# A fourth raw tile, later weight stores, and a tile for the second token tile beside the output weights

## The chip, the cores and the metric

The kernel runs on one core of a Trainium2 chip. The core has five engines that run at the same time, each with its own stream of instructions: TensorE (PE in the profile) multiplies matrices, VectorE (DVE) and GpSimd (POOL) do elementwise work, ScalarE (ACT) evaluates functions and copies, SyncE (SP) issues most transfers. The transfers themselves are done by 16 DMA engines. The metric is the device time of one execution in microseconds, the median of several runs; less is better.

## The reference

One layer of a hybrid backbone on 2048 latent tokens of width 1024, with a context of 256 tokens in front. Everything is in 32-bit floating point. Cut to what matters here:

```python
ada = jnp.einsum('bd,lde->lbe', jax.nn.silu(c), w_ada) + b_ada[:, None, :]
sh1, sc1, g1, sh2, sc2, g2 = (m[:, None, :] for m in jnp.split(ada[l], 6, axis=-1))
...
hc = modulate(rmsnorm(xc, norm_mix[l]), csh1, csc1)
logf_f, k_f, logf_b, k_b, vc = hgrn2_gates(hc @ w_in[l][:, :3 * w], lb_f, lb_b, first)
hf_c = advance_state(h0, k_f, vc, jnp.cumsum(logf_f, axis=2))
hb_c = advance_state(h0, flip_t(k_b), flip_t(vc), jnp.cumsum(flip_t(logf_b), axis=2))

h = modulate(rmsnorm(x, norm_mix[l]), sh1, sc1)
o, _, _ = token_mixers(h @ w_in[l], lb_f, lb_b, first, hf_c, hb_c, *mix_args)
x = x + g1 * (o @ w_out[l])
h2 = modulate(rmsnorm(x, norm_ffn[l]), sh2, sc2)
x = x + g2 * conv_ffn(h2, w_up[l], conv_w[l], conv_b[l], w_down[l], rows)
return rmsnorm(x, norm_final)
```

`token_mixers` has two groups of four heads. One is a gated linear recurrence that runs over the tokens forward and backward, each direction starting from the state that the context leaves. The other is a gate unit: `gelu(u) * (W_s LN(gelu(v)) + b)` over chunks of 128 positions. Their outputs are joined and go through `w_out`.

## The kernel before

Products that need accuracy are made of three multiplications: each operand is split into a high part in the rounded format float32r and the rest (`split`, L131: a cast on ACT, a subtraction on DVE or POOL), and `mm3` (L136) multiplies high by high, high by low and low by high.

The kernel has three phases.

Phase one (L192 to L1162) makes the input projection, the recurrences and the gate unit. It takes the tokens in two halves of 1024 (`hh` 0 and 1). `run_banks` (L525) goes through a list of column tiles of `w_in`; each is a product of 128 columns by up to 512 tokens in one PSUM bank. The 512 KB of weights of a column tile are loaded into a *raw tile* (`raw_tile`, L214: 4 KB in each partition, three of them) by `load_raw` (L219), and split into `whi` and `wlo` by `split_w` (L224), for which there are two pairs. Between the multiplications of a bank, `slot` (L185) lets two queues of background tasks go on. A task is a generator; what it yields is the number of microseconds of PE time, by the planner's own estimate in `Tensor` (L54), after which it goes on. The queue `hg_q` holds the recurrences of the heads. The queue `bg_q` holds, one after the other: the normalising of x, `ada_block` for the rest of the modulation (L951), `w_out_ops` (L982), `conv_taps`, `w_down_ops` (L998), and at the end `load` in `open_wo` (L1136).

`w_out_ops` has 16 steps. Each takes a raw tile, loads half a row block of `w_out` (L991), yields 8.0, multiplies by the gate `g1` on DVE (L993), splits, stores the result in DRAM (L995), and yields 1.5. `w_down_ops` has 22 steps: load (L1006), yield 8.0, multiply (L1008), store (L1009), yield 2.0. Both share the raw tiles with the projection weights. Nearly all transfers of the kernel are issued by SP, in program order: where SP waits for the data of a store, or for a tile to come free, all later transfers wait behind it.

The last projection banks of phase one belong to the gate unit. Its last step, `both` (L682), multiplies on POOL (L685) and stores to `oT_d` in DRAM (L686). Before the last four banks, `open_wo` (L1127) empties the queues, closes the pool `ph` of the recurrence, and opens `pw` in its place. Its `load` fetches the joined outputs of token tile 0 (L1138) and the prepared output weights, half by half (L1144), and splits token tile 0 some 17 us of PE time later (L1147).

Phase two (L1273 to L1374) is the output projection over 16 token tiles of 128 tokens, with the residual and the second norm. Tile `t` needs its joined outputs fetched (`fetch_o`, L1313) and split (`split_o`, L1319), 48 multiplications into a pair of PSUM banks (`dbank`, L1192), and its rows of x (`fetch_x`, L1324). Before the loop, tile 1 is fetched (L1329) and then the first rows of x (L1330).

After it come the up-projection with the convolution, and the down-projection with the final norm. The last is the only place of `root` (L1719) with a column as its second operand (L1749): the rows' mean square and a constant are added on POOL, and the power -0.5 is taken. PSUM has eight banks; each phase lays its own pool over them, in the order in which tags are first asked for.

Of the kernel before, what the change touches and what calls it, by code (L numbers as in the profile page):

```python
# [18 lines left out]
P = 128  # L19
D = 1024  # L20
# [63 lines left out]
def tile_trunk(ctx, tc, x, c, cx, c_ctx, w_ada, b_ada, norm_mix, norm_ffn, w_in, hg_norm, sgu_g, sgu_b,  # L84
# [15 lines left out]
    ones = cst.tile([P, P], F32, name="ones")  # L100
    G.memset(ones, 1.0)
    ones_r = cst.tile([P, P], F32R, name="ones_r")
    nc.gpsimd.tensor_copy(ones_r, ones)
# [87 lines left out]
    with es1:  # L191
# [5 lines left out]
        wa = [p1.tile([P, NK, TH], F32, tag=t, name="wa", align_bytes=AL) for t in ("xl", "xh")]  # L197
# [16 lines left out]
        def raw_tile():  # L214
            return p1.tile([P, D], F32, tag="raw", name="raw", bufs=3)
# [98 lines left out]
        cll = ph.tile([P, NK, CTX], F32R, tag="Q", name="cl", align_bytes=AL)  # L314
# [86 lines left out]
        xl = p1.tile([P, NK, TH], F32R, tag="xl", name="xl", align_bytes=AL)  # L401
        xh = p1.tile([P, NK, TH], F32R, tag="xh", name="xh", align_bytes=AL)
# [388 lines left out]
        def hg(hh, h, F, K, qs, vt, sgt):  # L791
            Q = ph.tile([P, 2, TH], F32, tag="Q", name="Q", align_bytes=AL)
# [129 lines left out]
        def deferred(h):  # L922

            Qb = ph.tile([P, 2, TH], F32, tag="Q", name="Qb", align_bytes=AL)[:, 0, :]
# [57 lines left out]
        def w_out_ops():  # L982

            for n in range(2):
                cl = slice(n * 512, n * 512 + 512)
                g = pm.tile([P, 512], F32, tag="acc", name="g1")
                ld(g, g_d[0:1, cl].broadcast_to([P, 512]))
                for k in range(NK):
# [5 lines left out]
                    split(hi.bitcast(F32R), w.bitcast(F32R), w, V)  # L994
                    st(wo_d[:, k, :, cl], raw)  # L995
                    yield 1.5

        def w_down_ops():  # L998

            for n in range(2):  # L1000
# [3 lines left out]
                for j in range(NF // 2):  # L1004
# [3 lines left out]
                    pin(V.tensor_mul(raw, raw, view(g, 0, [[0, 2], [1, 512]])))  # L1008
                    st(wd_d[j][:, :, cl], raw)  # L1009
                    yield 2.0  # L1010
# [116 lines left out]
        def open_wo():  # L1127
# [5 lines left out]
            first_o.append(lambda: pw.tile([P, 2, NK, P], F32R, tag="o", name="o", align_bytes=AL))  # L1133
            early = len(wo)

            def load():  # L1136
                raw = raw_tile().rearrange("p (k c) -> p k c", c=P)
                ld(raw, oT_d[0][:, :, 0:P])  # L1138
                for k in range(early, NK):
                    wo.append(pw.tile([P, 2, D], F32R, name=f"wo{k}", align_bytes=AL))  # L1140
                for n in range(2):
                    sl = slice(n * 512, n * 512 + 512)
                    for k in range(early, NK):
                        ld(wo[k][:, :, sl].bitcast(F32), wo_d[:, k, :, sl])  # L1144
                yield 17.0
# [717 lines left out]
```

## Time and profile before

| | |
|---|---|
| median of three runs | 2440.84 us (2436.05 to 2441.05) |
| the profiled execution | 2440.39 us |
| its span in the profile | 2438.6 us |
| time moved by DMA, mean over the span | 163 GB/s |
| first multiplication of phase two | 973.57 us after the start of the span |

The page gives each engine's busy time within the span, and the chain of work that ended last. A row of the timeline has the start and the duration in microseconds, the engine, the line, the operation, the tile written and those read, and in square brackets how long the engine had been idle and what ended it. A row of the windows has a stretch of time, its length, then the busy time and the number of instructions of PE, of its weight loads, of DVE, ACT and POOL, then the granted clock of TensorE (1.00 is full speed), the share of the DMA engines' time in use, and the GB/s moved. A row of the waits has who waited for whom, the sum in microseconds, how often, and the longest. A multiplication takes about 0.39 us from its start to its end and overlaps the next; one of 512 columns starts about 0.23 us after another.

### The profile page before, as it was taken

How to read it: one execution, taken by the hardware profiler on the slowest of the kernel's cores; microseconds unless marked ns; L12 is line 12 of the kernel's file. 1: busy time of each engine (PE TensorE's matmuls, PEld its weight loads, DVE VectorE, ACT ScalarE, POOL GpSimd, SP SyncE). 2: the span in 40 equal slices, each digit the busy share in tenths (PEclk: the TensorE clock that was granted, in tenths of full speed). 3: DMA queues.
4: the chain of work that ended last, by engine and by line, in shares of the span. 5: the costliest groups of instructions: out<-in, count | busy, mean ns of one | idle time of the engine just before them, and what ended most of it. 6: DMA issues, size and time to landing. Idle time of an engine off the chain costs nothing.

```text
span 2438.6 us, 32286 instructions
## 1 busy us (share of the span) xinstructions
PE 2402.0 (99%) x11711; PEld 1995.0 (82%) x11711; DVE 1656.9 (68%) x2253; ACT 1043.2 (43%) x1802; POOL 867.8 (36%) x788
## 2 busy tenths in 40 slices
PE   8999999999999999999999999999999999999998
PEld 5887887888888888788888888888888887888887
DVE  5757795765786785465596666639866772776875
ACT  3654344444444443354554444434445442332343
POOL 0021110210121122000688778787888870000002
PEclk9999999999999999999999999999999999999999
DMA  8365445463355234668922322562222238934755
GB/s 302 117 206 169 148 143 168 153 234 111 114 195 173 88 103 160 223 208 264 303 80 90 96 81 91 179 235 97 86 94 85 88 112 336 324 121 147 229 152 198
DMA packets 305581, 396.43 MB, mean 163 GB/s; under 512 B 32633, under 2 KB 215681, under 8 KB 302349
## 3 DMA queue, kind: packets, MB, share of 16 engines
q1 hardware_dynamic: 302132, 393.61, 48.6%
q8 instruction: 92, 1.51, 0.3%
q10 hardware_dynamic: 3289, 0.76, 0.1%
q14 instruction: 68, 0.56, 0.1%
HBM read 285.18 MB, written 109.13 MB: 162 GB/s over the span
## 4 chain that ended last, share of the span: by engine, by line
PE 54%; issue 2%; DMA 1%; DVE 1%; POOL 1%; ACT 1%; SPq 0%; POOLq 0%; ACTq 0%; DVEq 0%
PE dn L65 20%; PE ux L65 19%; PE uz L65 14%; PE pj L65 0%; POOL ra L1722 0%; DMA raw<-in_x_dram 0%; POOL rr L1723 0%; PE ux L69 0%; DMA raw<-in_w_up_dram 0%; DMA yf<-yd 0%; PE uz L69 0%; DVE dn L1433 0%; DMA yd<-fl 0%; POOL Al L134 0%; DVE cv L1357 0%
## 5 line engine op out<-in xcount | busy, mean ns | idle before, releaser
L1433 DVE SCALAR_TENSOR_TENSOR dn<-gp,taps,dn 128x1024 f32<-128x1024 f32 x352 | 448.2, 1284 | 97.5 <-ACT dn L1430 93.1
L65 PE MATMUL dn<-thl,mhl 128*128 128x512 f32 x1680 | 381.5, 389 | 1.2 <-ACT thl L133 1.2
L65 PEld LDWEIGHTS dn<-thl,mhl 128*128 128x128 f32 x1680 | 315.0, 188 | 67.7 <-ACT thl L133 2.1
L134 POOL TENSOR_TENSOR Al<-raw,Ah 128x512 fp32r<-128x512 f32 x264 | 341.7, 1311 | 65.8 <-ACT Ah L133 41.5
L65 PE MATMUL pj<-xh,whi 128*128 128x512 f32 x896 | 362.3, 405 | 0.3 <-ACT whi L133 0.3
L65 PE MATMUL pj<-xh,wlo 128*128 128x512 f32 x896 | 351.1, 392 | 1.2 <-DVE wlo L134 1.2
L65 PE MATMUL pj<-xl,whi 128*128 128x512 f32 x896 | 351.7, 393 | 0.0
L133 ACT CAST Ah<-raw 128x512 fp32r<-128x512 f32 x264 | 162.9, 620 | 238.9 <-PE ux L65 133.1
L65 PE MATMUL ux<-xah,Ah 128*128 128x512 f32 x528 | 205.7, 390 | 0.3 <-ACT keep L1497 0.3
L65 PEld LDWEIGHTS pj<-xh,wlo 128*128 128x128 f32 x896 | 168.3, 188 | 37.5 <-DVE wlo L134 2.1
L65 PEld LDWEIGHTS pj<-xh,whi 128*128 128x128 f32 x896 | 168.7, 188 | 34.2 <-issue 3.5
L65 PEld LDWEIGHTS pj<-xl,whi 128*128 128x128 f32 x896 | 168.9, 189 | 30.0 <-DVE xl L253 0.2
L65 PE MATMUL dn<-wo,o 128*128 128x512 f32 x768 | 184.4, 396 | 2.6 <-ACT o L133 2.1
L65 PE MATMUL uz<-yf,Ah 128*128 128x512 f32 x704 | 174.0, 389 | 0.0
L65 PEld LDWEIGHTS dn<-wo,o 128*128 128x128 f32 x768 | 143.0, 189 | 32.8 <-ACT o L133 2.5
L591 POOL TENSOR_TENSOR K<-K,tot 128x512 f32<-128x512 f32 x40 | 62.9, 1572 | 299.9 <-DVE tot L521 154.6
L65 PE MATMUL ux<-yf,Ah 128*128 128x512 f32 x528 | 155.4, 389 | 0.0
L65 PEld LDWEIGHTS uz<-yf,Ah 128*128 128x128 f32 x704 | 132.1, 188 | 27.4
L65 PE MATMUL ux<-xah,Al 128*128 128x512 f32 x528 | 141.8, 390 | 1.0 <-POOL Al L134 0.9
L65 PE MATMUL ux<-xal,Ah 128*128 128x512 f32 x352 | 137.0, 389 | 0.0
L1722 POOL TENSOR_SCALAR ra<-ss 128x1 f32<-128x1 f32 x8 | 5.3, 662 | 360.4 <-ACT jk L1714 360.4
L134 DVE TENSOR_TENSOR wlo<-raw,whi 128x1024 fp32r<-128x1024 f32 x68 | 84.1, 1236 | 68.3 <-ACT whi L133 67.3
(341 smaller groups left out, 4452.7 us busy)
## 6 DMA issues: line engine op xcount, KB each, us to landing
raw<-in_w_up_dram SPq DMA_DIRECT2D x88, 512.0 KB, 3.6
mr<-m SPq DMA_DIRECT2D x85, 512.0 KB, 5.5
raw<-in_w_in_dram SPq DMA_DIRECT2D x68, 512.0 KB, 4.0
sT<-wd SPq DMA_DIRECT2D x88, 256.0 KB, 5.8
raw<-in_w_ada_dram SPq DMA_DIRECT2D x32, 512.0 KB, 4.6
yf<-yd SPq DMA_DIRECT2D x14, 1024.0 KB, 10.4
m<-cv SPq DMA_DIRECT2D x22, 544.0 KB, 2.7
raw<-in_w_down_dram SPq DMA_DIRECT2D x22, 512.0 KB, 4.0
```

Source lines behind the costliest of these rows:

```text
L65: return self.engine.matmul(out, lhsT, rhs, **kw)
L133: keep(S.copy(hi, raw))
L134: (eng or G).tensor_sub(lo, raw, hi.bitcast(F32))
L591: e.tensor_mul(view(K2, row * W + o, src), view(K, o, src), view(tot, t0, [[4, n], [ts, 2], [0, B]]))
L1433: V.scalar_tensor_tensor(out=cr, in0=gt[:, t // 3:t // 3 + RH, t % 3:t % 3 + GW], scalar=taps[:, t * NF + f:t * NF + f + 1], in1=cr, op0=A ...
L1722: G.tensor_scalar(out=a, in0=ss, scalar1=plus, scalar2=None, op0=ALU.add)
```

## The change

Phase one gets four raw tiles instead of three. `w_out_ops` and `w_down_ops` yield 3.0 between the last computation of a step and its store, and nothing after the store; `w_out_ops` also yields 4.0 before it loads the first half of the gate. `load` in `open_wo` fetches token tile 1 into a tile of its own in `pw`, right behind the output weights, and phase two takes it from there.

The rest makes room or follows from it. The float32 tile `ones` goes: `ones_r` is computed from `ident` (times 0, plus 1) and read as float32 where `ones` was. Tiles that had tags of their own share one tag with as many slots: `wa`, `xl` and `xh`; `whi` and `wlo`. Several tiles lose the alignment to 512 bytes. Ahead of phase two's banks one tile of `ux` and one of `dn` are asked for and not used, so that `ux` comes first in PSUM and `dn` behind it. `root` uses a tensor addition where its second operand is a column.

```diff
-    ones = cst.tile([P, P], F32, name="ones")
-    G.memset(ones, 1.0)
     ones_r = cst.tile([P, P], F32R, name="ones_r")
-    nc.gpsimd.tensor_copy(ones_r, ones)
+    nc.gpsimd.tensor_scalar(out=ones_r, in0=ident, scalar1=0.0, scalar2=1.0, op0=ALU.mult, op1=ALU.add)
+    ones = ones_r.bitcast(F32)
...
-        wa = [p1.tile([P, NK, TH], F32, tag=t, name="wa", align_bytes=AL) for t in ("xl", "xh")]
+        wa = [p1.tile([P, NK, TH], F32, tag="xx", name="wa", bufs=2, align_bytes=AL) for i in range(2)]
...
-            return p1.tile([P, D], F32, tag="raw", name="raw", bufs=3)
+            return p1.tile([P, D], F32, tag="raw", name="raw", bufs=4)
...
-            hi = p1.tile([P, NK, P], F32R, tag=f"whi{at}", name="whi", align_bytes=AL)
-            lo = p1.tile([P, NK, P], F32R, tag=f"wlo{at}", name="wlo", align_bytes=AL)
+            hi = p1.tile([P, NK, P], F32R, tag="ww", name="whi", bufs=4, align_bytes=AL)
+            lo = p1.tile([P, NK, P], F32R, tag="ww", name="wlo", bufs=4, align_bytes=AL)
...
             for n in range(2):
                 cl = slice(n * 512, n * 512 + 512)
+                if n == 0:
+                    yield 4.0
                 g = pm.tile([P, 512], F32, tag="acc", name="g1")
...
                     V.tensor_mul(w, w, g)
                     split(hi.bitcast(F32R), w.bitcast(F32R), w, V)
+                    yield 3.0
                     st(wo_d[:, k, :, cl], raw)
-                    yield 1.5
...
                     pin(V.tensor_mul(raw, raw, view(g, 0, [[0, 2], [1, 512]])))
+                    yield 3.0
                     st(wd_d[j][:, :, cl], raw)
-                    yield 2.0
...
                         ld(wo[k][:, :, sl].bitcast(F32), wo_d[:, k, :, sl])
+                raw1 = pw.tile([P, NK, P], F32, name="raw1")
+                ld(raw1, oT_d[0][:, :, P:2 * P])
+                first_o.append(raw1)
                 yield 17.0
...
+    for first in (xbank, dbank):
+        first()
...
-        raw_o = {1: fetch_o(1)}
+        raw_o = {1: first_o[1]}
         xts = {0: fetch_x(0)}
-        ops = {0: first_o[1]}
+        ops = {0: first_o[2]}
...
-        G.tensor_scalar(out=a, in0=ss, scalar1=plus, scalar2=None, op0=ALU.add)
+        if isinstance(plus, float):
+            G.tensor_scalar(out=a, in0=ss, scalar1=plus, scalar2=None, op0=ALU.add)
+        else:
+            G.tensor_add(a, ss, plus)
```

The other hunks drop `align_bytes=AL` from the tiles `cl`, `Q`, `Qb`, `o`, `wo`, `yst` and `edges`, and give `xl` and `xh` the shared tag `xx`.

More of the change, by code (lines that the diff above doesn't have):

```diff
@@ L791, in hg @@
         def hg(hh, h, F, K, qs, vt, sgt):
-            Q = ph.tile([P, 2, TH], F32, tag="Q", name="Q", align_bytes=AL)
+            Q = ph.tile([P, 2, TH], F32, tag="Q", name="Q")
             kd = Q[:, 0, :]
@@ L1139, in load @@
                 for k in range(early, NK):
-                    wo.append(pw.tile([P, 2, D], F32R, name=f"wo{k}", align_bytes=AL))
+                    wo.append(pw.tile([P, 2, D], F32R, name=f"wo{k}"))
                 for n in range(2):
```

16 lines of the change are left out of this document (8 added, 8 removed).

## The prediction, before the changed kernel was run

> **What bounds the kernel now.** I read the page first, then the windows of equal stretches, then who waited for whom on PE, then the timeline around each wait.
>
> ```profile
> span 2438.6 us, 32286 instructions
> PE 2402.0 (99%) x11711; PEld 1995.0 (82%) x11711; DVE 1656.9 (68%) x2253; ACT 1043.2 (43%) x1802; POOL 867.8 (36%) x788
> 0.00:60.00 60.00, 50.90 (x236) 31.37 (x237) 31.39 (x57) 23.44 (x42) 4.31 (x14) 0.91 0.87 305
> 400.00:500.00 100.00, 96.99 (x529) 82.65 (x528) 68.11 (x107) 42.85 (x72) 14.94 (x11) 1.00 0.45 147
> 960.00:1000.00 40.00, 36.95 (x168) 29.88 (x167) 13.32 (x33) 5.37 (x7) 6.17 (x7) 0.96 0.79 276
> 1300.00:1650.00 350.00, 350.00 (x1546) 289.91 (x1545) 215.12 (x213) 150.00 (x248) 279.74 (x238) 1.00 0.38 129
> ```
>
> PE is busy for 2402.0 of 2438.6 us, so all waits together are 36.6 us. The change leaves the multiplications alone, so its gain is bounded by those 36.6 us and by the clock (the number after POOL: 0.91 in the first 60 us, 0.96 around 960 to 1000). Most of the up-projection has no PE wait at all (350.00 of 350.00). The edits bear on two places: waits inside phase one (3.0 us of idle in 400 to 500 is the worst there) and the passage to the output projection at 973 us.
>
> The passage first, from the timeline and the windows:
>
> ```profile
> 964.35 7.24 SPq L1144 DMA_DIRECT2D wo<-wo_d  x9
> 973.43 2.95 SPq L686 DMA_DIRECT2D oT<-nt  x2
> 974.74 1.29 POOL L685 TENSOR_TENSOR nt<-nt,gu 128x512 f32<-128x512 f32 x1 [1.33 <-issue]
> 976.48 0.83 SPq L1316 DMA_DIRECT2D raw<-oT  x1
> 977.35 3.17 SPq L1326 DMA_DIRECT2D raw<-in_x_dram  x1
> 983.65 1.07 PE L65 MATMUL dn<-wo,o 128*128 128x512 f32 x4
> 985.70 1.04 ACT L133 CAST o<-raw 128x1024 fp32r<-128x1024 f32 x1 [12.15 <-DMA raw<-in_x_dram]
> 986.78 1.22 DVE L134 TENSOR_TENSOR o<-raw,o 128x1024 fp32r<-128x1024 f32 x1 [12.18 <-ACT o L133]
> 986.80 0.73 PE L65 MATMUL dn<-wo,o 128*128 128x512 f32 x2 [2.08 <-ACT o L133]
> 988.06 18.24 PE L65 MATMUL dn<-wo,o 128*128 128x512 f32 x73 [0.52 <-DVE o L134]
> ...
> 975.00:978.00 3.00, 3.00 (x15) 2.45 (x14) 0.00 (x0) 0.00 (x0) 1.03 (x1) 1.00 1.05 401
> 984.00:987.00 3.00, 0.92 (x5) 0.46 (x4) 0.22 (x1) 1.04 (x1) 0.00 (x0) 1.00 1.04 328
> 987.00:990.00 3.00, 2.48 (x7) 1.65 (x7) 2.14 (x2) 0.77 (x1) 0.00 (x0) 0.60 0.26 81
> 990.00:995.00 5.00, 5.00 (x21) 4.10 (x20) 1.22 (x1) 1.32 (x3) 0.00 (x0) 0.90 0.95 336
> ```
>
> Read it as a chain. SP issues nine loads of output weights, then has to wait at the gate unit's last stores (L686) for POOL's product, which ends at 974.74 + 1.29 = 976.03. Only then does it issue the load of token tile 1 (L1316, 976.48), behind transfers that keep the DMA engines full (share 1.05). Tile 0 runs out at 983.65 + 1.07 = 984.72. The cast of tile 1 starts at 985.70, so PE waits 2.08 + 0.52 = 2.60 us. The clock pays too: 0.60 over 3 us and 0.90 over 5 us lose 3 x 0.4 + 5 x 0.1 = 1.7 us. The passage costs 4.3 us.
>
> Phase one's waits that touch the raw tiles:
>
> ```profile
> 404.00 0.69 DVE L993 TENSOR_TENSOR raw<-raw,g 128x512 f32<-128x512 f32 x1 [7.38 <-DMA raw<-in_w_out_dram]
> 405.89 0.50 PE L65 MATMUL pj<-xh,wlo 128*128 128x512 f32 x1 [0.42 <-DVE wlo L134]
> 415.65 0.50 PE L65 MATMUL sc<-kl,ones_r 128*128 128x512 f32 x1 [1.99 <-DVE kl L800]
> 590.57 1.05 ACT L133 CAST whi<-raw 128x1024 fp32r<-128x1024 f32 x1 [4.29 <-DMA raw<-in_w_in_dram]
> 598.60 0.50 PE L65 MATMUL sc<-kl,ones_r 128*128 128x512 f32 x1 [0.76 <-DVE kl L800]
> ...
> SPq L1009 <- DVE raw L1008: 75.6, 20, 12.9
> SPq L995 <- DVE raw L134: 52.5, 14, 6.0
> SPq L1006 <- DMA wd<-raw: 35.8, 14, 4.6
> SPq L991 <- DMA wo_d<-raw: 21.2, 9, 4.0
> ```
>
> DVE stands 7.38 us on a late load of output weights, and 0.42 and 1.99 us of PE waits follow within 12 us. At 590 ACT stands 4.29 us on a late projection weight, and 0.76 us follow. The loads are late because SP stands at stores whose data is not made (L995, L1009), or because no raw tile is free until a store has landed (L991, L1006). These PE waits sum to 0.42 + 1.99 + 0.76 = 3.17 us.
>
> **The change part by part.** *Tile beside the output weights.* One load of 512 KB moves from behind L686 to right behind the nine weight loads, so it passes the two stores of 256 KB and POOL's product. It leaves SP some 4.5 us earlier (about 972 instead of 976.48), but arrival is set by what is queued. At the 401 GB/s of 975 to 978, the two stores it passes are 0.52 MB, or 1.3 us. Either the load's own arrival released the cast at 985.70, and then the new arrival is 984.4; or, as the row says, the x load right behind it did (another 0.52 MB), and then it is 983.1. The cast takes 1.04 us, and the low part is ready 1.22 us plus small gaps after it. With arrival at 984.4, high is ready at 985.47 (0.75 us late) and low at 986.75, where PE wants it two multiplications of about 0.23 us later, at 985.93 (0.82 late): 1.57 us of wait stay. With 983.1, high is in time and low is 0.27 us late. I take the middle, 0.9: the gain is 1.7 us, with ends at 1.0 and 2.3. The weight loads ahead lose nothing. The stores are delayed by one issue (0.83 us), and nobody reads them within the phase. What is late next is the x load, wanted after tile 0, and it was in time behind the same bytes.
>
> *The clock.* The 2.60 us of waits here were followed by half speed; the 1.99 us at 415.65 were not (clock 1.00 in 400 to 500). A wait of at most 1.57 us lies on the harmless side, so the 1.7 us return as well. Together the passage gives 3.4 us; ends 1.0 (clock still lost) and 4.3 (all).
>
> The Trainium skill, "TensorE: Matmul & The Clock Gate", section "What's actually happening", puts the drop behind an idle window of about 3.4 us. By that, 2.60 us would not be enough and the passage would return only its 1.7 us. The rows at 987 and 990 show the drop after less, so the measurement decides and the sum keeps the clock.
>
> *Fourth raw tile, later stores.* Each of the 16 output-weight steps goes from 8.0 + 1.5 to 8.0 + 3.0 of the planner's PE time, each of the 22 down-weight steps from 10.0 to 11.0, and 4.0 are put ahead: 24 + 22 + 4 = 50 us more.
>
> ```profile
> L1009 SPq DMA_DIRECT2D wd<-raw x22: 524/525/618, 570.5 to 818.0; - x22
> L1008 DVE TENSOR_TENSOR raw<-raw,g x22: 1211/1217/2310, 569.2 to 816.8; 128x1024 f32<-128x1024 f32 x22
> 895.55 2.02 PE L65 MATMUL sc<-Q,K 128*128 128x128 f32 x16 [0.73 <-DVE K L591]
> ```
>
> The last down-weight store moves from 818 to about 868, well before the 964 at which the output weights are fetched, so nothing waits for the end of it. In exchange SP meets data that is made: the mean wait at L995 is 52.5 / 14 = 3.75 us, and 3.0 us later most of it is over. With a fourth tile the next load need not wait for a store to land. If all three waits go, that is 3.17 us. At the other end, four or five DVE products of 1.22 us land in 818 to 868, where waits such as the 0.73 us at 895.55 exist already: 5 x 0.73 = 3.7 us lost, if each makes one. I take 2.0 us gained, nearer the first end, since the same products leave an earlier stretch that has waits too.
>
> *Small edits at nothing.* Shared tags for the weight halves, the ada tiles and x change no count of slots; `ones` loses one POOL instruction in the first 2 us, where PE goes on to wait for DMA. The bank order of the next phase moves a pair of banks.
>
> ```profile
> 2007.56 0.69 DVE L1514 TENSOR_TENSOR cv<-ux,cv 128x512 f32<-128x512 f32 x1 [1.41 <-PE ux L65]
> 2010.08 0.39 PE L65 MATMUL dn<-Ah,mhl 128*128 128x512 f32 x1
> 2433.04 0.50 POOL L1722 TENSOR_SCALAR ra<-oss 128x1 f32<-128x1 f32 x1 [1.56 <-ACT dn L1748]
> 2433.62 0.57 POOL L1723 TENSOR_TENSOR rr<-ra,mhalf 128x1 f32<-128x1 f32 x1
> ```
>
> If the ux banks come first, the down-projection's first bank is freed at 2007.56 + 0.69 = 2008.25, ahead of its first use at 2010.08: free; without that cover, at most DVE's 0.69. In the tail one POOL addition of 0.50 us becomes a tensor addition; between zero and the 0.57 of the row behind it, that is -0.50 to +0.07 us, once, since only the last tile's addition is exposed; I take 0. In the first 60 us the second weight load no longer needs a freed raw tile; PE there waits for ada loads ahead of it, so 0, with one shifted clock stretch of 1.7 us either way as bound.
>
> **Sum.** 3.4 + 2.0 = 5.4 us. The profiled execution took 2440.39 us, 1.8 more than its span, and stands 0.45 under the median of 2440.84. 2440.39 - 5.4 = 2435.0.
>
> **The rivals.** *A: the queue decides, the moved load gains next to nothing.* For it: the DMA share of 1.05 from 975 on. Against it: the 0.52 MB that are passed. If the wait stays near 1.6 us, the clock still drops, and phase one only trades waits, the gain is 0 to 1.5: 2439 to 2440.4, I say 2439.5. The Trainium skill, "DMA: Bandwidth & Descriptors", section "Queues, rings and completion order", says that each DMA engine takes up descriptors in ring order; by that rule, issuing 4.5 us earlier is worth only the bytes passed, which is this rival's ground. The row of the full queue agrees.
>
> *B: slower, by the background work that moves.* The products that moved into 818 to 868 sit in DVE's in-order queue ahead of the recurrence's level updates, and PE waits behind each. Price: five steps at the largest such wait seen, 1.99 us, is 10; less the passage's 3.4, +6.6: 2447. It decides from two lengthened waits per three steps on. For it: the wait on K at 895.55. Against it: the products that move leave a stretch where DVE is late as well.
>
> *C: slower, by turn-taking.* If the four shared weight slots are handed out in turn, not to whoever finds one free, a context bank's weights wait for the projection bank that is still to run.
>
> ```profile
> 20.02 1.53 PE L69 MATMUL mi<-ident,raw 128*128 128x128 f32 x12
> 21.39 0.60 PE L69 MATMUL sc<-ident,raw 128*128 128x128 f32 x4
> 21.51 1.23 DVE L134 TENSOR_TENSOR wlo<-raw,whi 128x1024 fp32r<-128x1024 f32 x1 [1.02 <-ACT whi L133]
> 22.77 4.51 SPq L221 DMA_DIRECT2D raw<-in_w_in_dram  x2
> ```
>
> Each place would cost a cast and a subtraction, 1.04 + 1.23 = 2.3 us, at about six places: 14, net +8: 2448. Against it: the load at 22.77 waited for the weights' tile (done at 22.74) and not for the older context tiles (done at 21.99), so slots are not taken by age.
>
> **How the numbers follow.** What can be told from no change is about 0.2%, or 4.9 us, near the spread of the runs shown (2436.05 to 2441.05); under 2435.9 counts as faster, over 2445.7 as slower. The forecast gets 0.57 and its own range is 2431 to 2438: full gains (4.3 + 3.2 + 1.7) make 2431.2, the smallest (1.0 + 1.4) 2438. Of its 0.57, 0.48 count as faster and 0.09 as the same. A gets 0.24, all the same; B 0.14, C 0.05, both slower. That makes faster 0.48, same 0.33, slower 0.19. The range is 2430 to 2442: it takes in A and leaves out the worst of B, and C.
>
> **What would show it.** In the changed profile the load of token tile 1 stands ahead of the L686 stores; the PE wait before the second tile is under 1.6 us and the clock stays at 1.00 through 987 to 995; SP's waits at the two weight stores shrink to a third, those for landed stores nearly vanish; the last down-weight store is at about 868; no PE wait over 1 us from 360 to 620. The prediction is wrong if the cast of tile 1 still starts after 985.3 relative to the same end of tile 0, or if new waits of more than 3 us in sum stand between 800 and 900.

## The result, and the profile after

| | before | after |
|---|---|---|
| median (21 runs each, in turn on one chip) | 2437.23 us (2433.95 to 2441.05) | 2443.07 us (2437.85 to 2446.20) |
| ratio of after to before, 95% interval | | 1.0023 (1.0017 to 1.0029) |
| the profiled execution, its time | 2440.39 us | 2440.89 us |
| its span | 2438.6 us | 2439.1 us |

The changed kernel is 5.8 us slower; in later comparisons the kernel before had medians of 2438.29 to 2439.50 us, against which it is 3.6 to 4.8. The two profiled executions differ by half a microsecond only: the one of before stands 3.2 us above its median, the one of after 2.2 below. Much of what makes one execution differ from the next is how many short stretches at half clock it meets: of the 33 executions of the kernel before that belong to the runs f1_nt to f4_three, those with a mean clock of 0.996 took 2440.6 us on average, those with 0.998 took 2436.6. One execution of f4_three below took 6249.92 us, and its median there is that of the ten others. The rows of after that answer to those of before, first from the page:

```profile
span 2439.1 us, 32274 instructions
PE 2402.4 (98%) x11711; PEld 1993.0 (82%) x11711; DVE 1658.8 (68%) x2253; ACT 1044.7 (43%) x1802; POOL 872.4 (36%) x787
```

and from the windows (the number after POOL is the clock):

```profile
0.00:60.00 60.00, 51.27 (x246) 31.57 (x247) 32.56 (x58) 23.43 (x42) 4.21 (x13) 0.94 0.92 316
400.00:500.00 100.00, 98.24 (x535) 83.91 (x534) 65.50 (x103) 41.52 (x69) 14.67 (x11) 1.00 0.44 144
987.00:990.00 3.00, 2.48 (x11) 1.91 (x11) 1.77 (x2) 1.20 (x3) 0.00 (x0) 1.00 0.32 124
1300.00:1650.00 350.00, 350.00 (x1546) 289.82 (x1545) 215.10 (x213) 150.44 (x248) 280.18 (x237) 1.00 0.38 129
```

The clock over the first 60 us is 0.94 against 0.91 before (60 x 0.03 = 1.8 us), and 1.00 against 0.60 over the 3 us from 987 (with the 0.90 behind it, the prediction's 1.7 us). So this execution was spared 3.5 us that other executions pay; without them the pair of traces says about +4.

Both programs have the same 11711 multiplications, and in the same order but for 248 places, most of them from 564 to 606 us, where multiplications of a projection and of a recurrence change places. So the start of a multiplication in one trace less the start of the same one in the other says, place by place, where time is lost. Worked out from the two traces, in us, after less before, by stage of the time before:

```
  0 to 380    380 to 676   676 to 925   925 to 1000   1000 to 1167    behind
  -1.66       -2.05        +3.44        -1.18         +1.94           +0.15
```

The first column is the clock at the start (the first multiplication starts 0.79 us later, since `ident` now is made behind a longer POOL instruction; most of that is gone 6 us later, in waits for DMA). 925 to 1000 is the passage to phase two with its first two token tiles, and has the 1.7 us of clock in it. Three things are left: phase one gains 2.05 us and gives back 3.44; the passage gains nothing but the clock (without its 1.7 us it is 0.5 us longer); and the second phase, without a single new long wait, runs 1.94 us longer.

The new waits of phase one, from the timeline of PE, and DVE's rows in front of the second:

```profile
412.33 0.50 PE L65 MATMUL sc<-kl,ones_r 128*128 128x512 f32 x1 [0.77 <-DVE kl L799]
701.94 0.50 PE L65 MATMUL sc<-knl,ones_r 128*128 128x512 f32 x1 [1.29 <-DVE knl L821]
883.07 0.49 PE L65 MATMUL sc<-knl,ones_r 128*128 128x512 f32 x1 [1.06 <-DVE knl L821]
...
694.74 1.22 DVE L800 TENSOR_TENSOR Q<-qs,F 128x1024 f32<-128x1024 f32 x1
695.88 1.22 DVE L1009 TENSOR_TENSOR raw<-raw,g 128x1024 f32<-128x1024 f32 x1
697.01 1.22 DVE L814 TENSOR_TENSOR K<-K,Q 128x1024 f32<-128x1024 f32 x1
701.20 1.28 DVE L821 TENSOR_TENSOR knl<-K,knh 128x512 fp32r<-128x512 f32 x2
```

All 22 instructions of line L1009 in one row (shortest, middle and longest in ns, first and last start in us):

```profile
L1009 DVE TENSOR_TENSOR raw<-raw,g x22: 1208/1218/2311, 608.0 to 896.6; 128x1024 f32<-128x1024 f32 x22
```

and SP's waits at the two weight stores (sum, times, longest):

```profile
SPq L1011 <- DVE raw L1009: 92.5, 20, 19.9
SPq L997 <- DVE raw L133: 54.1, 14, 6.3
```

A product of the down weights (L1009) stands on DVE right between two steps of the recurrence (L800, L814); everything behind it, `knl` at last, is 1.2 us later, and PE waits 1.29 us. The products of this line begin 39 us later than before (608.0 for 569.2) and end 80 us later (896.6 for 816.8).

The passage, from the timeline:

```profile
972.14 0.64 SPq L1147 DMA_DIRECT2D raw<-oT  x1
973.48 5.45 SPq L685 DMA_DIRECT2D oT<-nt  x2
974.43 1.29 POOL L684 TENSOR_TENSOR nt<-nt,gu 128x512 f32<-128x512 f32 x1 [1.35 <-issue]
979.02 0.43 SPq L1333 DMA_DIRECT2D raw<-in_x_dram  x1
985.33 1.04 ACT L132 CAST o<-raw 128x1024 fp32r<-128x1024 f32 x1 [12.08 <-DMA oT<-nt]
986.43 0.73 PE L65 MATMUL dn<-wo,o 128*128 128x512 f32 x2 [1.91 <-ACT o L132]
987.69 4.48 PE L65 MATMUL dn<-wo,o 128*128 128x512 f32 x18 [0.53 <-DVE o L133]
```

The load of tile 1 leaves at 972.14, ahead of the gate unit's stores (now L685). Yet the cast starts at 985.33, and what released it is named as the *store* `oT<-nt`. PE waits 1.91 + 0.53 = 2.44 us, where it waited 2.60.

### The profile page after: what moved, and what is told of

Its sections match the earlier page's. It is cut to its first block, busy times and chain, and to the rows that moved or that the text cites. A ratio compares the mean times of both kernels' runs of the same rounds, so it can differ in the third digit from the quotient of the medians.

```text
span 2439.1 us, 32274 instructions
## 1 busy us (share of the span) xinstructions
PE 2402.4 (98%) x11711; PEld 1993.0 (82%) x11711; DVE 1658.8 (68%) x2253; ACT 1044.7 (43%) x1802; POOL 872.4 (36%) x787
## 5 line engine op out<-in xcount | busy, mean ns | idle before, releaser
L65 PEld LDWEIGHTS pj<-xh,wlo 128*128 128x128 f32 x896 | 168.3, 188 | 36.6 <-DVE wlo L133 1.2
```

What stands on the lines that cost most here:

```text
L65: return self.engine.matmul(out, lhsT, rhs, **kw)
```

## Experiments

All runs below are in groups of four that share their runs of the kernel before; 11 or 12 runs of each (10 of f4_three). "After" is the changed kernel, 2443.07, with a ratio of 1.0023. The kernel before moved from 2437.23 us beside it to 2438.29 to 2439.50 in the groups, so a difference of some 2 us between medians of different groups shows little by itself; the ratios and the traces say more.

| label | median, us | before in its group | ratio, 95% interval |
|---|---|---|---|
| e1_align | 2441.46 | 2438.29 | 1.0013 (1.0004 to 1.0021) |
| e2_o32 | 2442.89 | 2438.29 | 1.0016 (1.0007 to 1.0024) |
| e3_yields | 2437.73 | 2438.29 | 0.9996 (0.9986 to 1.0006) |
| e4_fetch | 2442.28 | 2438.29 | 1.0014 (1.0006 to 1.0023) |
| f1_nt | 2441.02 | 2438.81 | 1.0008 (1.0000 to 1.0017) |
| f2_hold | 2440.41 | 2438.81 | 1.0013 (1.0005 to 1.0022) |
| f3_all | 2434.51 | 2438.81 | 0.9986 (0.9977 to 0.9994) |
| f4_three | 2440.31 | 2438.81 | 1.0005 (0.9995 to 1.0014) |
| g1_down | 2439.82 | 2438.69 | 1.0006 (0.9997 to 1.0015) |
| g2_out | 2438.50 | 2438.69 | 0.9998 (0.9989 to 1.0007) |
| g3_banks | 2434.50 | 2438.69 | 0.9982 (0.9973 to 0.9991) |
| g4_late | 2436.38 | 2438.69 | 0.9989 (0.9980 to 0.9998) |
| h1_yst | 2435.16 | 2439.50 | 0.9982 (0.9973 to 0.9991) |
| h2_yst | 2439.32 | 2439.50 | 0.9996 (0.9987 to 1.0005) |
| h3_owo | 2441.37 | 2439.50 | 1.0009 (1.0000 to 1.0017) |
| h4_yst | 2439.47 | 2439.50 | 1.0001 (0.9992 to 1.0010) |

And the same stages as above for each, start of the multiplications less that in the profiled kernel before; the last column is, over the third to the last token tile, what the distances of the multiplications exceed 226.5 ns by, in sum (in every kernel a part of it lies at the norm's transposes, so the differences count):

```
            380-676  676-925  925-1000  1000-1167   distances
before        0        0        0         0           2.47
after       -2.05    +3.44    -1.18     +1.94         4.42
e1_align    -2.11    +3.87    -0.67     +1.70         2.43
e2_o32      -2.37    +3.29    +0.07     +0.78         3.29
e3_yields   -3.60    -0.02    -0.71     +1.40         4.44
e4_fetch    -2.22    +3.51    -1.16     +1.50         4.47
f1_nt       -2.28    +3.28    -2.18     +2.20         4.43
f2_hold     -0.03    -0.05    -1.33     +1.78         4.44
f3_all      -3.73     0.00    -3.46     +1.87         2.44
f4_three    -1.60    +0.45    +0.73     +1.36         4.42
g1_down     -2.38    +1.75    +0.97     +2.42         4.47
g2_out      -2.76    +1.47    -1.66     +1.53         4.46
g3_banks    -3.21    -0.03    -3.68     +0.81         2.41
g4_late     -2.97    -0.04    -1.78     +0.95         2.43
h1_yst      -2.73    -0.04    -3.40     +1.27         2.41
h2_yst      -1.70    +4.11    -2.21     +0.97         2.36
h3_owo      +1.57    +0.08    +3.28     +1.54         4.39
h4_yst      +1.19    +0.08    -0.78     +0.17         2.40
```

How far such a number varies from execution to execution is seen where nothing was changed: h3_owo and h4_yst have the phase one of before, and lie 1.57 and 1.19 us apart from it in 380 to 676, but within 0.1 in 676 to 925. Each of the two met a half-clock stretch of 1.7 us there, at 416 and 414 us, as f2_hold did at 415; without it they would be 0.1 and 0.5 us ahead of it. 925 to 1000 has one half-clock stretch in before, e1_align, e2_o32, f4_three, g1_down and h4_yst, two in h3_owo, and none in the others.

### Where the operands lie: e1_align, e2_o32

The hunks that drop `align_bytes` move tiles. In bytes modulo 512, as the built programs place them: before, `wo` and `o` all at 0; after, wo0 to wo2 at 0, wo3 to wo7 at 32, `o` at 32 for even token tiles and 128 for odd ones. e1_align puts all of them back to 0 by small unused tiles, e2_o32 only moves the odd `o` to 32. The edit of e2_o32 (e1_align has 96 in the place of 104, and three more such tiles in `p1` and `pw`):

```diff
+        po.tile([P, 104], F32, name="pad3")
```

> The changed kernel with the second phase's operands (all o, all wo) back on addresses that are multiples of 512; nothing else. In the changed kernel wo0 to wo2 lie at 0, wo3 to wo7 at 32, o at 32 (even token tiles) and 128 (odd ones) modulo 512, and the first multiplications of the second phase start 231 to 238 ns apart where 227 are the usual. Theory 'place': the place of the operands in SBUF sets that distance. Then 227 ns return in most of the second phase, the second phase (991 to 1190 us) gives back 2.2 us against the changed kernel, and the nine weight loads run a little faster; the time is 2.5 us below the changed kernel's, near 2440.5. Rival 'banks': the order of the PSUM banks sets it; then the distances stay and nothing is gained.

> The changed kernel with only the odd token tiles' o moved from 128 to 32 modulo 512, so that o and wo3 to wo7 share one offset that is no multiple of 512. Theory 'same offset': what matters is whether the two operands of a multiplication share an offset modulo 512; then odd tiles become like even ones (227 ns at wo3 to wo7, 232 to 235 at wo0 to wo2), some 90 ns a tile-and-position sum, 0.7 us in all. Theory 'multiple of 512': each operand off a multiple of 512 costs by itself; then odd tiles stay slow throughout and the gain is 0.

Measured, median ns from one multiplication's start to the next, three for each of wo0 to wo7, first half of an even and an odd token tile:

```
           even tile (third)                        odd tile (fourth)
before    227 227 227 227 227 227 227 227     233 227 226 235 230 232 227 227
after     232 235 232 227 227 227 227 227     231 230 237 235 234 234 234 238
e2_o32    235 235 232 227 227 227 227 227     230 231 233 231 233 227 227 226
e1_align  227 227 227 227 227 227 227 227     227 227 227 235 231 233 227 226
```

(230 to 235 right behind the norm's transposes, at the fourth to sixth weight of the odd tile, occurs in every kernel. In most of the later even tiles of after, the first four or five multiplications at the fourth and fifth weight also still take 229 to 236 ns, although both operands are at 32 there; behind them it is 227 in every tile, and in e2_o32 only one is late so.) The even tile of after decides between the two theories, and e2_o32 confirms it: where both operands are at 32 the distance is 227, as good as both at 0; where one is at 0 and the other at 32, or one at 128, it is 230 to 238. So it is a common offset that counts, not a multiple of 512. (The offsets seen are 0, 32, 96 and 128; a rule modulo 256 would fit them as well.) e2_o32 gained 4.42 - 3.29 = 1.1 us of distances, 1.16 of stage time. The Trainium skill, "SBUF — State Buffer", section "A bandwidth-pool intuition that's wrong (but worth ruling out)", gives TensorE a second, independent read port for weight loads. It says nothing of the operands' places; that they would not matter is what one might read from it, and the rows show that here they do.

The time answers less clearly than the distances: e1_align gained all 2.0 us of them, but only 0.24 us of the stage. What came in their place are PE waits of 0.27, 1.00 and 0.78 us on rows of the second norm (0.39 once in before). What it gains besides sits in the passage: -0.67 has 1.7 us of half clock in it, which after's -1.18 has not, so it is 1.2 us ahead of after there (h4_yst and before, which are alike in the passage, differ by 0.78). The weights' loads run faster in it. Windows while the queue is full of output weights, for before, after, e1_align and h3_owo:

```profile
971.00:975.00 4.00, 4.00 (x23) 3.47 (x22) 2.01 (x3) 0.60 (x2) 2.48 (x2) 1.00 1.05 407
```

```profile
971.00:975.00 4.00, 4.00 (x24) 3.41 (x23) 1.69 (x2) 0.60 (x1) 2.65 (x2) 1.00 1.05 391
```

```profile
973.00:977.00 4.00, 4.00 (x23) 3.48 (x22) 2.26 (x3) 0.60 (x1) 2.14 (x1) 1.00 1.05 408
```

```profile
971.00:975.00 4.00, 4.00 (x24) 3.43 (x23) 3.15 (x3) 1.60 (x2) 1.29 (x1) 1.00 1.04 390
```

407 and 408 GB/s into tiles at 0, 391 and 390 into tiles at 32. Over the 4 us around the first multiplication of phase two, the ten kernels with tiles at 32 have 387 to 393, the eight with all at 0 have 404 to 409, but for g3_banks with 396. Nine loads of 0.52 MB take 0.5 us longer so. The Trainium skill, "DMA: Bandwidth & Descriptors", section "How a descriptor splits into AXI transactions", has a transfer that does not start at a multiple of 256 bytes begin with a transaction from the multiple below it; by that rule 2048 bytes that start 32 past a multiple make nine transactions instead of eight, which is an estimate from the page. It speaks of the reading side, here it is the side written, but the rows go the same way, by 3 to 5%.

### The times of the background weights: e3_yields, f2_hold, f4_three, g1_down, g2_out

e3_yields is after with the old times (the diff below); f2_hold stores later but keeps the length of a step (no 4.0; 1.5 and 2.0 ahead of the stores, nothing behind them); f4_three is e3_yields with `bufs=3` for the raw tiles; g1_down has the old times for the down weights alone, g2_out for the output weights alone.

```diff
-                if n == 0:
-                    yield 4.0
...
-                    yield 3.0
                     st(wo_d[:, k, :, cl], raw)
+                    yield 1.5
...
-                    yield 3.0
                     st(wd_d[j][:, :, cl], raw)
+                    yield 2.0
```

> The changed kernel with the stores of the background weights at their old times (no 4.0, no 3.0 ahead of the stores, 1.5 and 2.0 behind them); four raw tiles stay. Theory 'moved products': the last down-weight products, moved by 50 us into 818 to 868, make the new PE waits on knl at 702, 873 and 883 us; then these go, the multiplications' starts at 925 us are 2 to 3.5 us earlier than in the changed kernel, less what the later stores had gained from 380 to 620 (up to 2.5 us): 0 to 2 us below the changed kernel. Rival 'tiles': the fourth raw tile or the other places cause them; then the waits at knl stay and the time is the same or longer by the 2 us.

> The changed kernel with the stores of the background weights 1.5 and 2.0 us of PE time after their products, but with the length of each step as it was before (9.5 and 10.0, no 4.0 ahead), so that the products stay where they were. Theory 'moved products': what cost 3.4 us from 700 to 925 was the products' new places, not the later stores; then the time is that of the kernel with the old times (2437.7) or up to 1 us less. Rival 'later stores': a store that leaves later holds a raw tile longer, and the loads of projection weights behind it on SP are late; then new waits on raw tiles appear from 380 to 620 and the time is 2439 to 2443.

> The changed kernel with the old times of the background weights and three raw tiles instead of four. Theory 'fourth tile': the 3.4 us by which the multiplications are ahead of the kernel before at 700 us come from the fourth raw tile; then they go, and the time is near 2441. Rival 'rest': the shared tags of the weight halves and of x make them; then they stay, near 2437.7.

> The changed kernel with the down weights' stores at their old times and the output weights' stores at the new ones. It splits the 5.3 us between the two helpers. Theory 'the down products are in the way': their new spacing puts them ahead of the recurrence's products on DVE; then PE's waits on knl at 702 and 883 us go, the waits before 560 us (0.77 on kl at 412, 0.46, 0.49) stay, and the time is 3 to 3.5 us below the changed kernel, near 2439.7. Rival 'the shift counts': the output weights' later end (some 39 us) shifts the down products into other places by itself; then waits over 1 us stay or come at other places from 650 to 925 and the time is 2441 to 2443.

> The other half: the changed kernel with the output weights' stores at their old times and the down weights' at the new ones. By 'the down products are in the way' the wait on kl at 412 goes (1.4 us from 380 to 620 come back) and waits on knl of 1 us each stay between 650 and 925: 2441 to 2442. By 'the shift counts' the late waits go too: 2438 to 2439.

e3_yields takes 5.3 us off, more than expected: the 3.44 us from 676 to 925 go entirely, and 1.55 more from 380 to 676. The same place on its DVE, without the down product between L800 and L814:

```profile
691.20 1.22 DVE L800 TENSOR_TENSOR Q<-qs,F 128x1024 f32<-128x1024 f32 x1
692.33 0.68 DVE L736 TENSOR_TENSOR on<-on,rk 128x512 f32<-128x512 f32 x1
692.93 1.24 DVE L814 TENSOR_TENSOR K<-K,Q 128x1024 f32<-128x1024 f32 x1
...
697.21 1.29 DVE L821 TENSOR_TENSOR knl<-K,knh 128x512 fp32r<-128x512 f32 x2
```

SP's wait at the output weights' store is shorter there than in before (52.5 us) and after (54.1):

```profile
SPq L994 <- DVE raw L133: 35.8, 12, 5.8
```

f2_hold separates the two effects of a later store. Its products stay where they were, and 676 to 925 shows no loss (-0.05). But the gain before 676 is gone too, -0.03 for e3_yields' -3.60, and the rows of its timeline name a reason for most of it:

```profile
409.44 0.34 SPq L990 DMA_DIRECT2D raw<-in_w_out_dram  x1
412.40 0.69 DVE L992 TENSOR_TENSOR raw<-raw,g 128x512 f32<-128x512 f32 x1 [1.91 <-DMA raw<-in_w_out_dram]
414.29 0.50 PE L65 MATMUL sc<-kl,ones_r 128*128 128x512 f32 x1 [2.02 <-DVE kl L799]
```

and the window behind them:

```profile
414.00:418.00 4.00, 3.71 (x10) 2.95 (x11) 3.96 (x6) 1.34 (x3) 0.00 (x0) 0.61 0.13 51
```

The next load of a step comes behind the store in the program; the later store makes it late (409.44), DVE stands 1.91 us at it, PE waits 2.02 us for `kl` behind it, and in this execution the clock falls to 0.61 (4 x 0.39 = 1.6 us of the loss, which is chance as much as cause: before had a wait of 1.99 us here and kept its clock). In e3_yields that load leaves at 405.13, and PE has no wait at this place. So both theories hold a part: later stores cost the load behind them, and longer steps move products into the recurrence.

f4_three shows what the fourth tile does: without it 2.0 us of the gain before 676 are missing (-1.60 for -3.60, neither with a half-clock stretch there), since PE waits of 1.31 and 0.76 us on `kl` at 414 and 597, which e3_yields has not, are back; its median is 2.6 us more, in another group. What makes the 1.60 that is left is not shown. g1_down and g2_out split the loss from 676 to 925 almost evenly: each keeps one wait near 700 (1.57 us on `on`, 1.12 us on `knl`), and the waits at 873 and 883 need both shifts: the last down product comes at 856.1 in g1_down and 842.1 in g2_out, and only in after at 896.6. Neither theory was right for both kernels: the wait near 700 comes with either shift, as "the shift counts" has it, while g1_down's time is that of the other theory.

### What holds tile 1: e4_fetch, f1_nt

e4_fetch is after with the load of tile 1 back behind the stores (the first two lines of the diff); f1_nt is after with two unused tiles of `nt` asked for first, so that `nt` lies low in `pm` (the last two).

```diff
-                ld(raw1, oT_d[0][:, :, P:2 * P])
...
+        ld(first_o[1], oT_d[0][:, :, P:2 * P])
...
+        for i in range(2):
+            pm.tile([P, 512], F32, tag="nt", name="nt0", bufs=2)
```

> The changed kernel with the load of token tile 1 (into its new tile) issued where it was before, behind the gate unit's last stores. Theory 'queue': the bytes queued set its arrival, and issuing it earlier is worth almost nothing; then the cast of tile 1 starts 0 to 0.6 us later than in the changed kernel relative to the end of tile 0. The prediction's step had 1.0 to 2.3 us for it.

> The changed kernel with the gate unit's product nt moved to another place in phase one's memory, so that the second token tile's o in phase two no longer lies over it; nothing else. Theory 'memory': in the changed kernel the cast of tile 1 waits for the gate unit's last store to finish, since that store reads memory in which o is to be written, and the early load only delayed this store. Then the cast starts when its own load has landed, 0.8 to 1.5 us sooner after the end of tile 0, PE's waits there fall from 2.44 to 1.0 to 1.6 us, and the half clock at this place goes: 1 to 3 us in all. Rival 'queue': the transfers in flight set it; then the waits stay at 2.4 us and the store remains as what released the cast only by coincidence.

With the load back behind the stores, the cast starts 1.18 us after the start of tile 0's last multiplication; in after 1.19. The move was worth nothing in this pair: in after it is the store that sets the start, in e4_fetch the load stands behind the stores again (its row names the load of x rows next to it). f1_nt says why. Phase two's `o` for odd tiles lay over phase one's `nt` (bytes 141952 to 150144 over 146208 to 150304), so the cast that writes it has to wait until the store has read `nt`, and the early load in front had made that very store later: the second one leaves at 978.54 us in after and at 976.05 in before. The overlap itself is not new. In the kernel before, `o` lay at 143360 to 151552 over `nt` at 144544 to 148640; there tile 1's own load stood behind the stores and had to come after them anyway. With `nt` elsewhere:

```profile
972.96 0.56 SPq L1149 DMA_DIRECT2D raw<-oT  x1
985.44 1.04 ACT L132 CAST o<-raw 128x1024 fp32r<-128x1024 f32 x1 [11.11 <-DMA raw<-oT]
986.53 0.73 PE L65 MATMUL dn<-wo,o 128*128 128x512 f32 x2 [0.93 <-ACT o L132]
987.79 6.59 PE L65 MATMUL dn<-wo,o 128*128 128x512 f32 x27 [0.53 <-DVE o L133]
```

Now the load itself releases the cast, and the wait is 0.93 + 0.53 = 1.46 us instead of 2.44; the ratio to before is 1.0008 instead of 1.0023. The size of one such wait proves little: in the nine kernels with `nt` under `o` and the load in front it is 0.76 to 3.15 us, and h4_yst, with the passage of before, has 1.64 for 2.60. Against the rival "queue" stand the releaser, which is tile 1's own load in all five kernels with `nt` away and in none of those nine (four name the store, five the load of x rows right behind it), and the kernels with all operands at 0: with `nt` away (f3_all, g3_banks, h1_yst below) the waits are 0, 0.53 and 0 us, with `nt` under `o` (e1_align, h2_yst, which also keep the new times) 1.77 and 1.87.

### All together, and the small edits: f3_all, g3_banks, g4_late

f3_all is after with the old times, `o` and `wo` at 0 and `nt` out of the way; it keeps the fourth raw tile and the early load. g3_banks is f3_all without the two banks asked for ahead of phase two, g4_late is f3_all with the load of tile 1 behind the stores.

> The changed kernel with the old times of the background weights, the second phase's operands on multiples of 512 bytes, and nt out of the way of tile 1's o: the four findings so far put together. If they add up: phase one 3.4 us ahead of the kernel before, the second phase at its old pace, the passage with a PE wait under 1 us and full clock; 2437.6 less 2.0 for the pace and 1.2 to 1.7 for the passage: 2434, some 4 us below the kernel before. If the waits at the passage come from what PE reaches too early, the 1.2 to 1.7 do not come: 2435.5.

> The kernel of all findings (f3_all) without the two banks asked for ahead of phase two, so that dn comes first in PSUM as in the kernel before. The prediction had this order at nothing. If so, the time is 2434.5 within 1 us and the starts of the multiplications differ by under 0.3 us after the passage; by the rival that the order matters, the passage or the change to the up-projection differs by 0.5 us or more.

> The kernel of all findings (f3_all) with the load of token tile 1 issued behind the gate unit's last stores, where it was before the change. In the changed kernel this place was worth nothing, since the store held the tile's memory. Theory 'memory first': with that memory free the place is worth what the prediction had, 1.0 to 2.3 us of PE wait, and the half clock on top in some executions: 2435.5 to 2438. Rival: it is still worth nothing, 2434.5.

f3_all beats both kernels: 2434.51 us, 0.9986 (0.9977 to 0.9994) of before. Tile 1 comes without any wait of PE:

```profile
971.65 22.71 PE L65 MATMUL dn<-wo,o 128*128 128x512 f32 x99 [0.94 <-DVE nt L722]
980.13 1.05 ACT L132 CAST o<-raw 128x1024 fp32r<-128x1024 f32 x1 [9.67 <-DMA raw<-oT]
```

The first 99 multiplications of phase two are one row: tile 0 (48) and all of tile 1 without a gap. g3_banks has the same median; the bank order is worth nothing that the median shows. g4_late loses 1.9 us of median and 3.46 - 1.78 = 1.7 in the passage, with PE waits of 0.51 + 0.53 us before tile 1 and no half clock: with the memory free, the early load is worth about what the prediction had put on it.

### The rest of the second phase: h1_yst, h2_yst, h3_owo, h4_yst

Open was why the second phase kept 1.7 us of its loss in e1_align and 1.87 in f3_all. `yst` had lost its alignment as well (192). h1_yst puts it back in f3_all, h2_yst in e1_align; h4_yst takes it alone off in the kernel before, h3_owo `o` and `wo` alone (32, 96). One line of h3_owo's diff; those for `wo` and for the odd `o` are alike, and h4_yst's for `yst` and `edges`:

```diff
# h3_owo, against before
-            first_o.append(lambda: pw.tile([P, 2, NK, P], F32R, tag="o", name="o", align_bytes=AL))
+            first_o.append(lambda: pw.tile([P, 2, NK, P], F32R, tag="o", name="o"))
```

> The kernel of all findings (f3_all) with yst, from which the second norm's results are stored, on a multiple of 512 again (it lies at 192 modulo 512 there). Theory 'stores': the stores from yst take longer from there, ACT's next step waits for them, and PE's waits on the norm's rows (1.47, 0.36 and 0.22 us in f3_all) follow; then these waits fall below 0.5 us in sum, the third to last token tile take about 167.4 us instead of 169.0, and the time is 2433. Rival 'phase': the waits come from where the planner's times put the norm's steps and differ from one execution to the next; then nothing changes beyond 0.5 us.

> The changed kernel with o, wo and yst on multiples of 512 (e1_align and yst): the lost alignment undone where the second phase uses it. By 'stores' the second phase takes what it took in the kernel before (within 0.4 us; e1_align was 1.7 longer) and the time is 2440, 1.5 under e1_align. By 'phase' it stays at 2441.5.

> The kernel before with o and wo alone off: wo3 to wo7 and the even tiles' o at 32, the odd tiles' o at 96, wo0 to wo2 at 0 modulo 512. Theory 'same offset': the distances grow as in the changed kernel (2.0 us in sum from the third tile on), the loads of the output weights are slower, and the time is 1.5 to 2.5 us over the kernel before: 2440 to 2441. Rival: with yst in place the second phase has slack elsewhere; then the distances grow and the time does not.

> The kernel before with yst (and the edges that share its tag) alone off, at 192 modulo 512 as in the changed kernel. By 'stores' waits on the norm's rows of 1 to 2 us in sum appear in the second phase and the time is 1 to 2 us over the kernel before: 2440. By 'phase' nothing changes: 2438.6.

`yst` is not it: alone off in before it adds 0.17 us to the stage and nothing to the median, and put back in f3_all it changes nothing beyond the spread. h2_yst's median is 2.1 us under e1_align's, in another group, but its waits on the norm's rows still sum to 1.39 us; of the 4.5 us between the two profiled executions, 1.7 are the half clock that its passage was spared. What makes the medians differ is not shown. `o` and `wo` account for the loss of the changed kernel itself: alone off in before they add 4.39 - 2.47 = 1.9 us of distances, 1.54 of stage, and make tile 1 later:

```profile
987.71 1.04 ACT L133 CAST o<-raw 128x1024 fp32r<-128x1024 f32 x1 [13.74 <-DMA raw<-oT]
988.80 0.74 PE L65 MATMUL dn<-wo,o 128*128 128x512 f32 x2 [3.21 <-ACT o L133]
990.06 5.49 PE L65 MATMUL dn<-wo,o 128*128 128x512 f32 x12 [0.52 <-DVE o L134]
```

3.73 us of wait for 2.60 (1.64 in h4_yst, where they are in place), and 1.9 us of median over its group's before. But in e1_align and f3_all they are in place, so they do not answer what was open. That stays open: the waits on the norm's rows (0.39 and 0.64 us in before and h4_yst; 1.2 to 2.05 in the variants of after with `o` and `wo` in place). They come and go between kernels that do not differ there (f3_all and g4_late have 1.87 and 0.95 us in this stage); that it is where the planner's times put the norm's steps is a guess, and a cause was not found.

## Why the prediction was wrong, step by step

**The sum as a whole.** It forecast 5.4 us less; the pair of traces, without its luck with the clock, has 4.0 more. Of the 9.4 us between, the passage makes 3.9 (0.5 longer for 3.4 shorter), phase one 3.4 (1.39 longer for 2.0 shorter) and the second phase 1.94, for which the sum had no term. The sum also started from an execution of 2440.39 us, 3.2 above the median of 21, so that 2435.0 stood only 2.2 us under the kernel before; that flattered the number and touches no mechanism.

**What bounds the kernel.** PE and its clock do. But "the change leaves the multiplications alone, so its gain is bounded by those 36.6 us" took their distance as given. The edits that drop the alignment were in the diff and were put at nothing without a reason; they are the largest missing term: 1.9 us of distances (shown alone by h3_owo) and a slower load of the weights.

**The moved load (1.7 us predicted).** 2.60 - 2.44 = 0.16 measured. The step that failed: "The stores are delayed by one issue (0.83 us), and nobody reads them within the phase." The second store left 2.5 us later, and though nobody reads the stores, a tile is laid over what they read from (f1_nt). The size of the estimate was about right: with that memory free and the weights in place the move was worth 1.7 us (g4_late against f3_all). Its first sign of being wrong came true: the cast starts at 985.33, and tile 0's last multiplication 0.2 us earlier than before, so relative to the same end of tile 0 it is still after 985.3. And in f1_nt 1.46 us of wait stayed, close to the 1.57 that the sum had for an arrival behind the queued bytes.

**The clock (1.7 us predicted).** "A wait of at most 1.57 us lies on the harmless side" took the length of a wait for what decides. It does not: waits of 1.09 + 0.52 = 1.61 us before tile 1 cost the clock in f4_three, 2.44 us did not in after. (No run here lost it at this place after less than 1.61.) The profiled pair shows the predicted 1.00 at 987 by chance, not by the change.

**Fourth raw tile, later stores (2.0 us predicted).** Up to 676 us the size came out, 2.05, but that is luck in part: with the fourth tile and the old times 3.60 are gained and the waits of 3.17 us that the prediction had summed are gone, as it said they might be (e3_yields); the fourth tile makes 2.0 of it (f4_three), and the new times take 1.55 away. "3.0 us later most of it is over" failed: the waits at the two stores are 92.5 and 54.1 us where 75.6 and 52.5 were. A longer step makes the data later too, but that is not the whole of it: f2_hold, with later stores and no longer steps, has 74.9 and 39.4, where e3_yields has 74.0 and 35.8. So a later store in the program did not find its data readier; why is not shown. The shift was mis-sized too: 80 us at the end instead of 50, so the last product is at 896.6 and not at 868.

**The small edits** at nothing: right for the banks (g3_banks, by the median) and `ones` (most of its 0.79 us vanish in 6 us); the addition in `root` was not tested alone, and from the second phase to the end 0.15 us is all that is added.

**The rivals.** B had the mechanism, DVE's products ahead of the recurrence, and put it in 818 to 868 at 10 us; it is 3.44 us, at 702, 873 and 883, and "less the passage's 3.4" did not come. A had the passage's outcome, with the queue as its ground, where the memory was. C did not occur: up to 380 us the changed kernel is 1.66 us ahead, about what its clock gives it. The time left the range by 1.1 us at its upper end, by two losses of which one was given a small chance and the other no term.

## What to carry to other kernels

Where a change moves a transfer ahead of others, look up what lies where in memory: a tile laid over the source of a store waits for that store, and a transfer put in front of the store makes the wait longer, even where the overlap is old. An attribute such as an alignment that is dropped "to make room" is an edit with a price; compare the distance of multiplications between the two traces even where no wait shows. And a background step that is made longer moves all steps behind it: before lengthening, find which engine its work stands on at its new place, and who is in line behind.

## What the runs showed of the hardware

- Two operands of a multiplication at different offsets modulo 512 bytes: 230 to 238 ns from start to start instead of 227 at 128x512 (0 with 32, 96 or 128; 32 with 96 or 128); equal offsets, 0 or 32, 227, though up to five multiplications right behind unequal ones still take 229 to 236.
- Loads of 2048-byte rows into tiles 32 bytes past a multiple of 512: 387 to 393 GB/s with the queue full instead of 404 to 409 (one kernel of eight 396).
- The half clock came after PE waits of 1.61 us in one execution and did not come after 2.44 us in another, at the same place of the program. The rows of the first, f4_three, from the timeline and the windows:

```profile
986.12 0.74 PE L65 MATMUL dn<-wo,o 128*128 128x512 f32 x2 [1.09 <-ACT o L132]
987.38 6.96 PE L65 MATMUL dn<-wo,o 128*128 128x512 f32 x22 [0.52 <-DVE o L133]
```

```profile
988.00:992.00 4.00, 4.00 (x12) 3.17 (x11) 1.69 (x2) 2.08 (x3) 0.00 (x0) 0.57 0.68 204
```
